# The queries' rotary sine part added in DRAM by accumulating transfers, in a retention and attention block on one core

## The chip, the cores and the metric

The kernel runs on one core of a Trainium2 chip. The metric is the device time of one execution in microseconds (us): the median of three runs is 1068.7 us, the lowest 1065.72, the highest 1070.0. A core has a matrix engine (PE, which loads its weights beside its products, PEld), a vector engine (DVE), an activation engine (ACT), a general engine (POOL) and a queue engine that only issues transfers (SP). Sixteen DMA engines move data between DRAM and the core's memory. POOL can issue transfers too, through a software queue, and of the kernel's transfers only those add to what stands at the destination.

## The reference

One encoder block over 1024 positions and 16 learned tokens ahead of them, in float32. One input projection feeds two branches, and a gated sum of both goes through an output projection and a norm:

```python
u = _rms_norm(h, pre_w)
z = u @ w_in
rq, rk, rv, rg, aq, ak, av, ag, gr, ga = _split_in(z)
...
o_r = _bidirectional_retention(rq, rk, rv, lg_f, lg_b)[:, META_PAD:]
...
o_r = o_r * ret_nw.astype(jnp.float32) * jax.nn.silu(rg.astype(jnp.float32))
y_r = o_r.astype(h.dtype) @ w_rb

aq = _pad_front(_rotary(aq.reshape(B, T, ATT_HEADS, ATT_HD), pos))
ak = _pad_front(_rotary(ak.reshape(B, T, ATT_GROUPS, ATT_HD), pos))
...
o_a = _windowed_sink_attention(aq, ak, av, sink)[:, META_PAD:].reshape(B, T, ATT_Q)
o_a = o_a * jax.nn.silu(ag.astype(jnp.float32))
y_a = o_a.astype(h.dtype) @ w_ab

mix = jax.nn.sigmoid(gr) * y_r + jax.nn.sigmoid(ga) * y_a
out = mix @ w_o
return h + _rms_norm(out, post_w)
```

The change concerns the rotary of the attention's queries, `aq`: 8 heads of 128 channels.

```python
t1, t2 = tf[..., :half], tf[..., half:]
return jnp.concatenate([t1 * cos - t2 * sin, t2 * cos + t1 * sin], axis=-1)
```

Each half of a head's channels, 64 of 128, gets the other half times the sine.

## The kernel before

A float32 product is made of three products of rounded parts: an operand is cast on ACT to its high part, DVE subtracts that from the operand to get the low part, and `mm3` (L94 to L96) issues high x high, low x high and high x low. So nearly every weight tile costs one ACT cast and one DVE subtraction (L110) ahead of its matmuls.

The large projections run in "phases" (class `Phase`). A phase works through units of 256 output channels by 1024 positions, by a scheme of seven products in place of eight (`PROD`): `prepare` makes the sums of weight blocks and splits them (for the first phase in rows of L1011, L1033 and L110, tiles `why`, `wly`, `wry`), `product` issues twelve matmuls into a PSUM bank, `combine` adds the banks' results into four output tiles `c1`, `u2`, `u3`, `c5` of 128x512, and a `post` works on each finished tile.

The stages, in us of the profiled execution: the retention's projections and the retention itself up to about 330; the first phase `y` to about 515, with units 0 and 1, then 16 and 17, 18 and 19 (the attention's queries), then 2 and 3; the attention to 666; and then the phases `z` (remaining gates), `r`, `a` and `o`. In the first phase the posts of units 0 to 3 multiply a gate into the retention's result (`z_post`, L1320, L1330, L1333; it loads the result as tile `v`, L1314), and those of units 16 to 19 are `query_post` (L1443): two DVE products of 64 partitions each write the sine part with its halves swapped into a tile `m2` (L1446, L1447), a third makes the cosine part (L1448), POOL adds the two (L1449), and SP stores the sum to `aq_d` in DRAM (L1451). There are 16 such posts, four for each unit. The attention loads the queries back from `aq_d` (`qf`).

Beside the phases runs helper work that later stages need: single products of "prepared" units (`LATER`: 4, 10, 5, 11, ...), whose weights come by `pre_fetch` (L850, tiles `we`, two of 512 KB), are summed by `pre_sums` (L855; DVE rows L860 to L862) and split by `pre_parts` and `pre_low` (tiles `w_4h`, `w_4l`, `w_10h`, `w_10l`). `gen_pre` makes the products (banks `pe`), copies them to a tile `e` (L885) and stores it; `pre_split` (L814, L822, L825) makes sums of `w_out` as tiles `wT..` and stores them. Tables of numbers set where in the order this work is written down: `FIRST_AT` by steps of the first phase (F is `pre_fetch`, S `pre_sums`, P `pre_parts`, L `pre_low`, then the unit), `BEGUN` by steps of the attention's helper products, `FILL` how many of those stand between the parts of each attention chunk, `REFILL` and `LATE` loads and splits of the last phases. A scheduler with a model of time then orders the instructions of each engine.

Two rings of buffers matter. The ring `g` (`gtile`, 7 tiles of 128x512 in the first phase, 6 later) holds the tiles `v`, `e` and `wT`; `m2` has 2 of its own. The weight tiles `wr` come in two pairs, one in the pool `keep`, one in `lp`; `pre_fetch` takes the pair in `keep`.

A chunk of the attention goes from the scores on PE (`ps`) through DVE (L1523) and ACT (L1526) to POOL, which divides (tile `p`, L1536), and back to PE for transposes (`pt`, L1547) and values (`po`).

Of the kernel before, what the change touches and what calls it, by code (L numbers as in the profile page):

```python
# [7 lines left out]
F32 = mybir.dt.float32  # L8
R = mybir.dt.float32r
AF = mybir.ActivationFunctionType  # L10
ALU = mybir.AluOpType
# [5 lines left out]
P = 128  # L17
# [7 lines left out]
MW = 720  # L25
NC = 2 * NB
START = 4, 12
FILL = ((2, 2),) * 1 + ((2, 1),) * 1 + ((2, 3),) * 2 + ((4, 3),) * 1 + ((2, 3),) * 6 + ((2, 4),) * 1 + ((2, 3),) * 1 + ((2, 4),) * 1 + ((2, 3),) * 1 + ((3, 3),) * 1 + ((2, 1),) * 1 + ((2, 2),) * 1 + ((2, 3),) * 2 + ((2, 4),) * 1 + ((0, 3),) * 1 + ((2, 3),) * 4 + ((3, 3),) * 1 + ((2, 4),) * 1 + ((1, 3),) * 1
EARLY = 8, 9
LATER = 4, 10, 5, 11, 6, 12, 7, 13, 14, 15  # L30
PRE = {u: (2, 3, 5) for u in LATER}
BORDER = 12, 0, 12
LAST = 9
REFILL = -48, 5, 5
LATE = -15, -14, -13, -9, -7, -6, -5, -3, -3, -1

LEADS = 2, 4, 6
VALUES_AT = ((-1, "w1", "s0", "s1"), (1, "l2"), (4, "w0"), (6, "c2"), (8, "n6", "s2", "pT2.0.1.2"),
             (16, "f0", "l3"), (17, "f1", "f2"), (20, "c3", "z"), (21, "s3", "f3"), (22, "pT2.3"))
FIRST_AT = ((1, "k6"), (2, "pT3"), (6, "pT4"), (7, "m4"), (12, "tT3"), (13, "x0"), (14, "tT2", "tT4"),  # L40
# [4 lines left out]

U_QK, U_V, U_G = 0, 4, 8
U_AK, U_AV, U_AQ, U_AG = 12, 13, 14, 18
# [8 lines left out]
def block_kernel(ctx: ExitStack, tc: tile.TileContext, xT, x, meta, w_in, w_rb, w_ab, w_out, vecs, dec, sink,  # L56
                 post_w, rope, tab, out):
    nc = tc.nc
    PSUM = bass.MemoryType.PSUM

    keep = ctx.enter_context(tc.tile_pool(name="keep", bufs=1))
# [37 lines left out]
    def follow(*ins):  # L99

        st = ExitStack()
        for i in ins:
            st.enter_context(tc.issue_after(i))
        return st
# [92 lines left out]
    sr = turn.tile([P, T], F32, name="sr")  # L197
# [320 lines left out]
    z_stack, lp = ExitStack(), None  # L518
# [204 lines left out]
    aq_d = [dram.tile([4, P, SEQ], F32, tag=f"aq{g}", name=f"aq_d{g}") for g in range(2)]  # L723
# [110 lines left out]
    fetched_w, parts = {}, {}  # L834
    spare, e_from, e_bank = [ra], [pj], {}
# [12 lines left out]
            parts[u, 2] = part(h, i), part(l, i)  # L848

    def pre_fetch(u):  # L850
        fetched_w[u] = [keep.tile([P, 4, 256], F32, tag="wr", bufs=2, name=f"we{u}_{j}") for j in range(2)]
        for j, t in enumerate(fetched_w[u]):
            nc.sync.dma_start(t, w_in[gates[u], :, 4 * j:4 * j + 4, :])

# [115 lines left out]
    final = "o", 3, 4  # L970
    sub, mul, add = ALU.subtract, ALU.mult, ALU.add

    staged, gates_ = [2, 6], [7]

    def stage(name, j=0, dt=F32):
        return (yp if j else lp).tile([P, 512], dt, tag=f"sg{int(j)}", bufs=staged[bool(j)], name=name)
# [1 line left out]
    def gtile(name):  # L978
        return gp.tile([P, 512], F32, tag="g", bufs=gates_[0], name=name)
# [205 lines left out]
    def refill(nm, src):  # L1185
# [3 lines left out]
        def load(i, j):  # L1189
            def f():  # L1190
                for k in range(4):
                    x[i, j, k] = t = stage(f"{nm}{i}{j}{k}", j)
                    src(t, 4 * i + k, j)
            return f
# [4 lines left out]
        def plain(n, i, j):  # L1199
            def f():  # L1200
                for k in range(4):
                    split_b(n, k, x[i, j, k])
            return f
# [23 lines left out]
        def early(k):  # L1227
            def f():
                a, b, c, d = (stage(f"{nm}e{i}{j}{k}", j) for i in range(2) for j in range(2))
                for t, (i, j) in zip((a, b, c, d), ((0, 0), (0, 1), (1, 0), (1, 1))):  # L1230
                    src(t, 4 * i + k, j)
                x["e", k] = a, b, c, d
            return f

        def split_early(k):
            def f():
                a, b, c, d = x.pop(("e", k))
                nc.vector.tensor_tensor(a, b, a, sub)
                for n, t in (("T1", a), ("B21", c), ("B22", d)):
                    split_b(n, k, t)  # L1240
            return f
# [10 lines left out]
        if nm == "z":  # L1252
            d = {}
            for i, f in zip(LATE, (load(0, 1), load(1, 1), load(0, 0), t23, plain("B11", 0, 0), load(1, 0),
                                   plain("T2", 1, 1), plain("T3", 0, 1), t4, plain("T4", 1, 0))):
                d.setdefault(i, []).append(f)
            for k in range(4):
                d.setdefault(REFILL[0] + REFILL[1] * k, []).insert(0, early(k))
                d.setdefault(REFILL[0] + REFILL[1] * k + REFILL[2], []).append(split_early(k))
            return d  # L1260
# [181 lines left out]
    ph_o = Phase("o", seq, o_load, o_post, apart=(0, 1))  # L1442
    def query_post(u, i, j, o, to=None):  # L1443
        s, to = half[j], o if to is None else to
        m2 = spare[0].tile([P, 512], F32, tag="m2", bufs=2, name=f"m2_aq{u}{i}{j}")
        nc.vector.tensor_tensor(m2[64:128], o[0:64], sr[0:64, s], mul)  # L1446
        nc.vector.tensor_tensor(m2[0:64], o[64:128], sr[64:128, s], mul)  # L1447
        nc.vector.tensor_tensor(to, o, cr[:, s], mul)  # L1448
        nc.gpsimd.tensor_tensor(to, to, m2, add)  # L1449
        made.add((u, j, i))  # L1450
        nc.sync.dma_start(aq_d[u // 2][2 * (u % 2) + i, :, 512 * j:512 * j + 512], to)  # L1451

    def first_post(u, i, j, o, to=None):
        (query_post if u > 15 else z_post)(u - 16 * (u > 15), i, j, o, to)
# [33 lines left out]
    def attention():  # L1488
# [95 lines left out]
        def fill(n):  # L1584
            owed[0] += n
            while owed[0] > 0:
                cost = next(works, None)
                if cost is None:
                    return
                owed[0] -= cost  # L1590
# [11 lines left out]
        def scores(k):  # L1602
            with follow(*latest, *marks("oa", "lo")):
                stage1(*chunks[k])
            if chunks[k] == (0, 2 * NB - 1):
                keys(1, 0, later_k[0][:, NM:NM + 256], later_k[0][:, 0:NM])
            if chunks[k] == (1, 0):
                keys(1, 1, later_k[0][:, NM + 256:T])
            edge_values(*chunks[k])
# [11 lines left out]
        for k in range(len(chunks)):  # L1621
# [9 lines left out]
            if ends > 0:  # L1631
                with follow(*latest):
                    fill(FILL[k][0])
                scores(k + 2)
                with follow(*latest):
                    fill(FILL[k][1])
            if k:
# [61 lines left out]
    def first_weights(u):  # L1699
        for n in ("A11", "A12"):  # L1700
            first_phase.block(u, n)

    jobs = dict(l=x_load, c=x_scale, s=x_sums, p=x_parts, f=x_first, t=t_store, m=more, n=second_fetch, k=second_parts, x=lambda k: pre_load(k, act_src(w_out)), y=pre_split, A=ready, F=pre_fetch, S=pre_sums, P=pre_parts,
                L=pre_low, z=lambda _: next(first), w=first_weights, r=lambda _: first_phase.raw.clear())

    def at(table):
        return {i: [(jobs[j[0]], *(int(a) if a.isdigit() else a for a in j[1:].split("."))) for j in js]
                for i, *js in table}
# [16 lines left out]
    free[:] = ["pj"] * 3 + ["p1"] * 2 + ["p3"]  # L1725
    table = at(FIRST_AT)
    for n, _ in enumerate(first):
# [9 lines left out]
    vah, val = (atv.tile([P, NB, 256], R, name=n) for n in ("vah", "val"))  # L1737

    BEGUN = {5: [(pre_sums, 5), (pre_fetch, 11)],
             6: [(pre_parts, 5)],  # L1740
             7: [(pre_low, 5)],
             13: [(pre_sums, 11), (pre_fetch, 6)],
             14: [(pre_parts, 11)],
             15: [(pre_low, 11)],
# [2 lines left out]
             23: [(pre_low, 6)],  # L1747
             24: [(load_k,)],
             29: [(pre_sums, 12), (pre_fetch, 7)],
             30: [(pre_parts, 12)],  # L1750
             31: [(pre_low, 12)],
             37: [(pre_sums, 7), (pre_fetch, 13)],
             38: [(pre_parts, 7)],
             39: [(pre_low, 7)],
# [13 lines left out]
    i = attention()  # L1768
# [7 lines left out]
    lp = ctx.enter_context(tc.tile_pool(name="lp", bufs=1, reuse_waits="tile", side="right"))  # L1776
# [105 lines left out]
```

## Time and profile before

| | |
|---|---|
| median of three runs | 1068.7 us (1065.72 to 1070.0) |
| profiled execution, its own time | 1067.16 us |
| its span | 1065.4 us |
| granted PE clock over the span | 0.993 |
| PE, DVE, ACT, POOL busy | 1033.8, 866.9, 510.5, 214.7 us |
| PE idle in 404 to 496, 496 to 532 | 8.62, 7.55 us |
| DVE busy in 404 to 496 | 90.50 of 92 us |
| DMA moved | 212.98 MB, of it 6.82 MB through the software queue |

Rows of instructions give the start, the duration, the engine, the line, the operation, the tiles written and read, and in brackets the idle time ahead of it with what ended it. Rows of waits give the waiting engine and tile, what it waited for, the total, how often, and the longest. Rows of windows give the stretch, its length and the busy time of each engine with the number of instructions, then the granted clock, the share of the DMA engines and GB/s. Rows of groups give shortest, median and longest duration in ns. PE's matmuls overlap, so that one of 0.40 us follows another by 0.23.

### The profile page before, as it was taken

Reading aid. Unit: us, or ns where it says so; the run is one execution under the profiler, and the core shown is the slowest. Engines: PE = TensorE matmul, PEld = TensorE weight load, DVE = VectorE, ACT = ScalarE, POOL = GpSimd, SP = SyncE. Lnnn points to the kernel's source line nnn. Section 1 sums busy time; section 2 is a strip of 40 time slices with the busy share of each in tenths; the row PEclk is TensorE's granted clock in tenths of the full one; section 3 lists DMA queues with packets and bytes.
Section 4 is the critical chain, followed back from the end, with each engine's and each line's share of the span. In section 5 each row is a group of like instructions: output and inputs, shape, how many; then the busy total and the mean of one; then the engine's idle time right before and its main releaser. Section 6 shows DMA issues by size and latency. Waiting matters only on the chain.

```text
span 1065.4 us, 17204 instructions
## 1 busy us (share of the span) xinstructions
PE 1033.8 (97%) x5797; PEld 893.1 (84%) x5797; DVE 866.9 (81%) x1750; ACT 510.5 (48%) x1116; POOL 214.7 (20%) x268
## 2 busy tenths in 40 slices
PE   9999999999999999998799999999999999999996
PEld 7998999989998888776588989788888888787885
DVE  7887778879899689997867886789899799768764
ACT  5541432423435642422567777466557445333443
POOL 3324225344242002221123322000000000111032
PEclk9999999999999999999999999999999999999999
DMA  9322212224343596583867684999989747789364
GB/s 339 150 80 90 99 41 80 80 84 155 100 150 120 183 397 241 186 267 119 294 210 230 210 259 137 351 368 358 319 274 351 259 140 236 217 221 324 98 99 80
DMA packets 115017, 212.98 MB, mean 200 GB/s; under 512 B 12160, under 2 KB 43808, under 8 KB 112304
## 3 DMA queue, kind: packets, MB, share of 16 engines
q1 hardware_dynamic: 111040, 204.78, 55.9%
q0 software_dynamic: 3744, 6.82, 4.4%
q8 instruction: 46, 0.75, 0.3%
q14 instruction: 43, 0.35, 0.1%
q10 hardware_dynamic: 144, 0.27, 0.1%
HBM read 142.57 MB, written 72.93 MB: 202 GB/s over the span
## 4 chain that ended last, share of the span: by engine, by line
PE 80%; DVE 9%; DMA 7%; issue 2%; ACT 1%; POOL 1%; SPq 0%; DVEq 0%; POOLq 0%; ACTq 0%
PE bz L95 5%; PE bz L94 5%; PE bz L96 5%; PE pv L95 3%; PE pv L94 3%; PE pv L96 3%; PE bo L95 2%; PE bo L94 2%; PE br L95 2%; PE bo L96 2%; PE br L94 2%; PE br L96 2%; PE by L95 2%; PE by L96 2%; PE by L94 2%
## 5 line engine op out<-in xcount | busy, mean ns | idle before, releaser
L94 PE MATMUL pv<-wh,big 128*128 128x256 f32 x256 | 73.3, 286 | 0.0
L95 PE MATMUL pv<-wh,big 128*128 128x256 f32 x256 | 72.9, 285 | 0.0
L96 PE MATMUL pv<-wl,big 128*128 128x256 f32 x256 | 72.5, 283 | 0.0
L1536 POOL TENSOR_SCALAR p<-p,den 128x352 f32<-128x352 f32 (+2 forms) x60 | 38.0, 646 | 127.6 <-DVE den L1529 54.8
L1368 POOL DMA_DIRECT2D mx_d<-c1a x4 | 3.7, 920 | 287.0 <-DVE c1a L1359 287.0
L1011 ACT CAST why<-wry 128x512 fp32r<-128x512 f32 x56 | 32.9, 620 | 57.9 <-DVE wry L1033 33.0
L94 PE MATMUL bz<-T,lhz 128*128 128x512 f32 x144 | 56.8, 395 | 0.0
L96 PE MATMUL bz<-T,lhz 128*128 128x512 f32 x144 | 56.8, 394 | 0.0
L95 PE MATMUL bz<-T,llz 128*128 128x512 f32 x144 | 56.8, 394 | 0.0
L94 PE MATMUL by<-big,why 128*128 128x512 f32 x128 | 51.0, 400 | 4.4 <-DVE c5y L1448 4.4
L95 PE MATMUL by<-big,wly 128*128 128x512 f32 x128 | 51.3, 401 | 0.0
L96 PE MATMUL by<-big,why 128*128 128x512 f32 x128 | 50.8, 397 | 0.0
L110 DVE TENSOR_TENSOR wly<-wry,why 128x512 fp32r<-128x512 f32 x56 | 43.7, 802 | 6.3 <-ACT why L1011 6.0
L95 PEld LDWEIGHTS pv<-wh,big 128*128 128x128 f32 x256 | 48.2, 188 | 0.3
L94 PEld LDWEIGHTS pv<-wh,big 128*128 128x128 f32 x256 | 48.2, 188 | 0.2
L96 PEld LDWEIGHTS pv<-wl,big 128*128 128x128 f32 x256 | 48.3, 189 | 0.2
L1526 ACT ACTIVATE p<-raw,nm 128x353 f32<-128x353 f32 (+2 forms) x64 | 36.2, 567 | 20.4 <-DVE nm L1523 19.5
L1523 DVE CUSTOM_DVE_ANT_0 raw<-ps,mask,nsink 128x352 f32<-128x352 f32 (+2 forms) x64 | 33.2, 548 | 3.0 <-ACT p L1526 1.6
L595 ACT ACTIVATE op<-pa,rcol 128x256 f32<-128x256 f32 x32 | 15.2, 476 | 42.0 <-PE pa L96 41.6
L657 ACT ACTIVATE ost<-to,rnw 128x128 f32<-128x128 f32 x64 | 20.0, 365 | 31.4 <-PE to L652 22.1
L687 POOL TENSOR_TENSOR rs<-rs,mhalf 128x1 f32<-128x1 f32 x32 | 23.3, 729 | 52.8 <-DVE rs L686 49.6
L94 PEld LDWEIGHTS by<-big,why 128*128 128x128 f32 x128 | 24.4, 191 | 10.7 <-ACT u2y L1105 4.8
(723 smaller groups left out, 3788.0 us busy)
## 6 DMA issues: line engine op xcount, KB each, us to landing
e<-e SPq DMA_DIRECT2D x60, 256.0 KB, 5.2
we<-in_w_in_dram SPq DMA_DIRECT2D x20, 512.0 KB, 5.1
wr<-in_w_in_dram SPq DMA_DIRECT2D x19, 512.0 KB, 4.3
wry<-in_w_in_dram SPq DMA_DIRECT2D x16, 512.0 KB, 6.4
tg<-tg_d SPq DMA_DIRECT2D x32, 256.0 KB, 5.1
T<-tT SPq DMA_DIRECT2D x6, 1024.0 KB, 10.8
T<-preT SPq DMA_DIRECT2D x6, 1024.0 KB, 7.6
wrz<-in_w_in_dram SPq DMA_DIRECT2D x20, 256.0 KB, 5.5
```

Source lines behind the costliest of these rows:

```text
L94: nc.tensor.matmul(o, ah, bh, start=first, stop=False, **kw)
L95: nc.tensor.matmul(o, al, bh, start=False, stop=False, **kw)
L96: latest[:] = [nc.tensor.matmul(o, ah, bl, start=False, stop=last, **kw).ins]
L110: return nc.vector.tensor_tensor(o, i, hi.bitcast(F32), ALU.subtract).ins
L595: nc.scalar.activation(o, pa[:, 0:256], AF.Copy, scale=rcol[:, c:c + 1])
L657: nc.scalar.activation(ost[0][:, e_, w0:w0 + P], to[:, P * e_:P * e_ + P], AF.Copy, scale=rnw[:, 2 * h + e_:2 * h + e_ + 1])
L687: nc.gpsimd.tensor_tensor(rs, rs, mhalf[:, 0:1], ALU.pow)
L1011: nc.scalar.copy(h, src)
L1368: nc.gpsimd.dma_start(d, to, accum_op=ALU.add)
L1523: nc.vector.tensor_tensor_reduce(raw[e_][:, 1:1 + wid], s[:, 0:wid], mask[:, mo:mo + wid], -SCALE, nsink[:, hp:hp + 1], ALU.add, ALU.min, ...
L1526: last["exp"] = nc.scalar.activation(p[:, 0:1 + wid], raw[e_][:, 0:1 + wid], AF.Exp, scale=-1.0, bias=nm_[:, e_:e_ + 1], accum_out=den[:, ...
L1536: nc.gpsimd.tensor_scalar(pt[e_][:, 0:wid], pt[e_][:, 0:wid], den[:, e_:e_ + 1], 1.0, op0=ALU.mult, op1=ALU.mult)
```

## The change

`query_post` now makes the sine part unswapped, in one DVE product over 128 partitions, into a tile of the ring `g`. The cosine part is stored to `aq_d` as soon as DVE has made it. POOL then issues two accumulating transfers of 64 partitions (128 KB) each, which add the upper half of the sine part to the lower half in DRAM and the other way round. POOL's adds are gone. The ring `g` has 9 tiles in the first phase. Unit 10's weights go into the pair `wr` of the pool `lp`, and are fetched beside unit 4's; the helper tables are renumbered.

```diff
-FILL = ...
+FILL = ...
-REFILL = -48, 5, 5
-LATE = -15, -14, -13, -9, -7, -6, -5, -3, -3, -1
+REFILL = -48, 6, 5
+LATE = -15, -14, -12, -9, -7, -6, -5, -3, -3, -1
...
-            (37, "y2.3"), (44, "A0"), (47, "m4"), (49, "r", "F4"), (51, "S4", "P4", "A1"),
-            (52, "L4", "F10", "A2"), (53, "A3"), (54, "m4", "S10", "P10", "L10", "F5"))
+            (37, "y2.3"), (44, "A0"), (47, "m4"), (49, "r", "F4", "F10"), (51, "S4", "P4", "A1"),
+            (52, "L4", "F5", "A2"), (53, "S10", "P10", "A3"), (54, "m4", "L10"))
...
     def pre_fetch(u):
-        fetched_w[u] = [keep.tile([P, 4, 256], F32, tag="wr", bufs=2, name=f"we{u}_{j}") for j in range(2)]
+        pool = lp if u == LATER[1] else keep
+        fetched_w[u] = [pool.tile([P, 4, 256], F32, tag="wr", bufs=2, name=f"we{u}_{j}") for j in range(2)]
...
-    staged, gates_ = [2, 6], [7]
+    staged, gates_ = [2, 6], [9]
...
     def query_post(u, i, j, o, to=None):
         s, to = half[j], o if to is None else to
-        m2 = spare[0].tile([P, 512], F32, tag="m2", bufs=2, name=f"m2_aq{u}{i}{j}")
-        nc.vector.tensor_tensor(m2[64:128], o[0:64], sr[0:64, s], mul)
-        nc.vector.tensor_tensor(m2[0:64], o[64:128], sr[64:128, s], mul)
+        m2 = gtile(f"m2_aq{u}{i}{j}")
+        nc.vector.tensor_tensor(m2, o, sr[:, s], mul)
         nc.vector.tensor_tensor(to, o, cr[:, s], mul)
-        nc.gpsimd.tensor_tensor(to, to, m2, add)
         made.add((u, j, i))
-        nc.sync.dma_start(aq_d[u // 2][2 * (u % 2) + i, :, 512 * j:512 * j + 512], to)
+        d = aq_d[u // 2][2 * (u % 2) + i, :, 512 * j:512 * j + 512]
+        nc.sync.dma_start(d, to)
+        for a, b in ((slice(0, 64), slice(64, P)), (slice(64, P), slice(0, 64))):
+            nc.gpsimd.dma_start(d[a], m2[b], accum_op=ALU.add)
...
-             30: [(pre_parts, 12)],
-             31: [(pre_low, 12)],
+             30: [(pre_parts, 12), (pre_low, 12)],
```

`FILL`, 32 pairs long, differs in four of them; not shown are two moves in `FIRST_AT`, "tT4" from step 14 to 12 and "k8" from 31 to 27.

PE has the same 5728 rows in another order, DVE 16 fewer, and POOL 32 transfers for 16 adds. The first place is DVE at the last three query posts of units 18 and 19. Before (`m_aq` is `m2`, `by` the bank, `wly` low parts of weights):

```order
L1446 TENSOR_TENSOR m_aq_6203<-by_1_5896,sr 64x512
L1447 TENSOR_TENSOR m_aq_6203<-by_1_5896,sr 64x512
L1448 TENSOR_TENSOR c5y_6202<-by_1_5896,cr 128x512
L110 TENSOR_TENSOR wly_6_6211<-wry_0_6129,why_6_6210 128x512
L110 TENSOR_TENSOR wly_7_6255<-wry_0_6102,why_7_6254 128x512
L1448 TENSOR_TENSOR u2y_6016<-u2y_6016,cr 128x512
L110 TENSOR_TENSOR wly_7_6255<-wry_0_6129,why_7_6254 128x512
L110 TENSOR_TENSOR wly_4_6294<-wry_1_6159,why_4_6293 128x512
L110 TENSOR_TENSOR wly_4_6294<-wry_1_6185,why_4_6293 128x512
L1446 TENSOR_TENSOR m_aq_6227<-by_1_5923,sr 64x512
L1447 TENSOR_TENSOR m_aq_6227<-by_1_5923,sr 64x512
L1448 TENSOR_TENSOR c5y_6226<-by_1_5923,cr 128x512
```

And now, with the same posts:

```order
L1447 TENSOR_TENSOR m_aq_6203<-by_1_5900,sr 128x512
L1448 TENSOR_TENSOR c5y_6202<-by_1_5900,cr 128x512
L110 TENSOR_TENSOR wly_5_6163<-wry_0_6129,why_5_6162 128x512
L1034 TENSOR_TENSOR wry_0_6102<-wry_0_6102 128x512
L1448 TENSOR_TENSOR u2y_6016<-u2y_6016,cr 128x512
L1447 TENSOR_TENSOR m_aq_6227<-by_1_5927,sr 128x512
L1448 TENSOR_TENSOR c5y_6226<-by_1_5927,cr 128x512
```

The posts now stand ahead of the splits of products 6, 7 and 4 of units 2 and 3, which stood among them.

The second place is SP's queue at the end of the query posts, up to the weights of unit 10 (6499 before, 6430 and 6431 now; unit 4's are 6426 and 6427). Before:

```order
L1451 DMA aq_d_587<-u2y_5997 128x512
L1451 DMA aq_d_587<-c5y_6202 128x512
L1451 DMA aq_d_587<-u2y_6016 128x512
L1451 DMA aq_d_587<-c5y_6226 128x512
L853 DMA we_0_6426<-in_w_in_dram 128x1024
L1304 DMA wx_7556<-in_w_out_dram 128x512 x2
L853 DMA we_1_6427<-in_w_in_dram 128x1024
L1304 DMA wx_7559<-in_w_out_dram 128x512 x2
L863 DMA s_4_100<-we_1_6427 128x512
L853 DMA we_0_6499<-in_w_in_dram 128x1024
```

And now:

```order
L1451 DMA aq_d_587<-c5y_6226 128x512
L1315 DMA v_6356<-oTr_d 128x512
L887 DMA e_2_94<-e_2_6373 128x512
L1315 DMA v_6395<-oTr_d 128x512
L1315 DMA v_6421<-oTr_d 128x512
L854 DMA we_0_6426<-in_w_in_dram 128x1024
L887 DMA e_2_97<-e_2_6578 128x512
L854 DMA we_0_6430<-in_w_in_dram 128x1024
L854 DMA we_1_6427<-in_w_in_dram 128x1024
L854 DMA we_1_6431<-in_w_in_dram 128x1024
```

Unit 10's weights are fetched among unit 4's, the loads `wx` come later, and loads of `v` and stores of `e` now stand between the last query store and the fetch. Through the ring `g`, the loads of `v` wait for accumulating transfers that read the buffer before.

The third place is ACT in the last products of units 2 and 3, before:

```order
L1105 COPY u2y_6354<-by_1_6258 128x512
L1011 CAST why_3_6398<-wry_1_6159 128x512
L1011 CAST why_3_6398<-wry_1_6185 128x512
L1105 COPY u3y_6388<-by_1_6236 128x512
L1105 COPY u3y_6414<-by_1_6258 128x512
L790 CAST w_4h<-we_0_6426 128x1024
```

and now:

```order
L1106 COPY u2y_6354<-by_1_6258 128x512
L1012 CAST why_2_6338<-wry_1_6185 128x512
L886 COPY e_2_6578<-pe_2_6565 128x512
L1012 CAST why_3_6398<-wry_1_6159 128x512
L1012 CAST why_3_6398<-wry_1_6185 128x512
L1106 COPY u3y_6388<-by_1_6236 128x512
```

The copy of the result `e_2_6578` now stands ahead of the casts of `why_3`; its buffer of the ring `g` is the one that the last query post's sine part leaves, so it waits for the last accumulating transfer.

More of the change, by code (lines that the diff above doesn't have):

```diff
@@ L27 @@
 START = 4, 12
-FILL = ((2, 2),) * 1 + ((2, 1),) * 1 + ((2, 3),) * 2 + ((4, 3),) * 1 + ((2, 3),) * 6 + ((2, 4),) * 1 + ((2, 3),) * 1 + ((2, 4),) * 1 + ((2, 3),) * 1 + ((3, 3),) * 1 + ((2, 1),) * 1 + ((2, 2),) * 1 + ((2, 3),) * 2 + ((2, 4),) * 1 + ((0, 3),) * 1 + ((2, 3),) * 4 + ((3, 3),) * 1 + ((2, 4),) * 1 + ((1, 3),) * 1
+FILL = ((2, 2),) * 1 + ((3, 1),) * 1 + ((2, 3),) * 1 + ((2, 2),) * 1 + ((4, 3),) * 1 + ((2, 3),) * 6 + ((2, 4),) * 1 + ((2, 3),) * 1 + ((2, 4),) * 1 + ((2, 3),) * 1 + ((3, 3),) * 1 + ((2, 1),) * 1 + ((2, 2),) * 1 + ((2, 3),) * 2 + ((2, 4),) * 1 + ((0, 4),) * 1 + ((2, 2),) * 1 + ((2, 3),) * 3 + ((3, 3),) * 1 + ((2, 4),) * 1 + ((1, 3),) * 1
 EARLY = 8, 9
@@ L39 @@
              (16, "f0", "l3"), (17, "f1", "f2"), (20, "c3", "z"), (21, "s3", "f3"), (22, "pT2.3"))
-FIRST_AT = ((1, "k6"), (2, "pT3"), (6, "pT4"), (7, "m4"), (12, "tT3"), (13, "x0"), (14, "tT2", "tT4"),
+FIRST_AT = ((1, "k6"), (2, "pT3"), (6, "pT4"), (7, "m4"), (12, "tT3", "tT4"), (13, "x0"), (14, "tT2"),
             (16, "y0.0"), (17, "y0.1"), (18, "y0.2"), (19, "y0.3", "x1"), (23, "y1.0"), (24, "m4", "y1.1"),
[3 rows of a table removed]
[3 rows of a table added]
 U_QK, U_V, U_G = 0, 4, 8
```

2 rows, old and new, of the table FIRST_AT are left out of this document.

## The prediction

> **What bounds the kernel now.** I read the page's busy times and chain first, then the windows stage by stage, then the waits, and last the rows around the longest waits.
>
> ```profile
> PE 1033.8 (97%) x5797; PEld 893.1 (84%) x5797; DVE 866.9 (81%) x1750; ACT 510.5 (48%) x1116; POOL 214.7 (20%) x268
> PE 80%; DVE 9%; DMA 7%; issue 2%; ACT 1%; POOL 1%; SPq 0%; DVEq 0%; POOLq 0%; ACTq 0%
> 404.00:496.00 92.00, 83.38 (x350) 65.81 (x349) 90.50 (x118) 28.91 (x51) 25.05 (x16) 0.98 0.57 193
> 496.00:532.00 36.00, 28.45 (x125) 22.28 (x124) 26.21 (x52) 16.18 (x31) 2.64 (x4) 0.95 0.81 272
> 536.00:666.00 130.00, 127.96 (x817) 115.41 (x816) 97.88 (x261) 93.25 (x255) 34.90 (x56) 1.00 0.66 206
> 666.00:990.00 324.00, 322.33 (x1394) 260.00 (x1393) 274.08 (x448) 168.51 (x305) 10.61 (x12) 1.00 0.84 283
> ```
>
> The window rows give length, then busy time of PE, PEld, DVE, ACT and POOL, the granted clock, the DMA share and GB/s. From 666 to 990 PE stands still for 1.67 us of 324, and in the attention for 2.04 of 130: the end moves one for one with PE, and there is nothing to win there. From 404 to 496, the stretch of the query posts, the roles change: DVE is busy for 90.50 of 92 us and PE idles for 8.62. From 496 to 532, the hand-over to the attention, PE idles for 7.55 more. After the two longest pauses the clock falls as well:
>
> ```profile
> 488.00:492.00 4.00, 0.56 (x1) 0.34 (x2) 3.94 (x7) 0.58 (x1) 0.59 (x2) 0.88 0.18 66
> 492.00:496.00 4.00, 4.00 (x14) 3.21 (x14) 3.86 (x5) 1.17 (x2) 1.02 (x1) 0.69 0.30 95
> 528.00:532.00 4.00, 1.66 (x6) 1.10 (x7) 3.10 (x10) 2.59 (x10) 2.64 (x4) 0.57 0.97 335
> 532.00:536.00 4.00, 4.00 (x16) 3.52 (x15) 3.19 (x8) 2.90 (x7) 0.46 (x1) 0.57 0.99 351
> 486.67 0.40 PE L94 MATMUL by<-big,why 128*128 128x512 f32 x1
> 491.44 0.76 PE L94 MATMUL by<-big,why 128*128 128x512 f32 x1 [4.38 <-DVE c5y L1448]
> PE by L94 <- DVE c5y L1448: 4.4, 1, 4.4
> PE by L95 <- DVE wly L110: 4.2, 4, 2.1
> PE pe L95 <- DVE w_10l L110: 2.4, 1, 2.4
> ```
>
> The work lost to the clock is busy time x (1 - clock): 1.2 us in 492 to 496 (4.00 x 0.31), 0.7 in 528 to 532 and 1.7 in 532 to 536. So 8.62 + 1.2 = 9.8 us can be won before 496, and 7.55 + 2.4 = 10.0 us in the hand-over. Nothing else in the kernel is within reach of this change.
>
> **What the posts cost DVE.** Sixteen query posts run here.
>
> ```profile
> L1446 DVE TENSOR_TENSOR m_aq<-c1y,sr x4: 685/685/1284, 401.7 to 456.0; 64x512 f32<-64x512 f32 x4
> L1447 DVE TENSOR_TENSOR m_aq<-c1y,sr x4: 686/687/689, 402.4 to 456.7; 64x512 f32<-64x512 f32 x4
> L1448 DVE TENSOR_TENSOR c1y<-c1y,cr x4: 683/684/693, 403.7 to 460.4; 128x512 f32<-128x512 f32 x4
> 413.01 0.68 DVE L1446 TENSOR_TENSOR m_aq<-u3y,sr 64x512 f32<-64x512 f32 x1
> 413.71 1.69 DVE L1447 TENSOR_TENSOR m_aq<-u3y,sr 64x512 f32<-64x512 f32 x1
> 413.12 1.74 POOL L1449 TENSOR_TENSOR u3y<-u3y,m_aq 128x512 f32<-128x512 f32 x1 [4.00 <-issue]
> L1449 POOL TENSOR_TENSOR u3y<-u3y,m_aq x4: 1290/1678/1741, 413.1 to 471.7; 128x512 f32<-128x512 f32 x4
> 405.02 1.28 DVE L1446 TENSOR_TENSOR m_aq<-c1y,sr 64x512 f32<-64x512 f32 x1
> 404.47 1.29 POOL L1449 TENSOR_TENSOR c1y<-c1y,m_aq 128x512 f32<-128x512 f32 x1 [57.57 <-DVE c1y L1448]
> ```
>
> (1) A product over 64 partitions lasts as long as one over 128 (0.685 beside 0.684). One instruction for two therefore takes 16 x 0.69 = 11 us off DVE. (2) Where a POOL add runs, the DVE instruction that meets it ends with it: 0.6 us late at 405.02, 1.0 at 413.71. At these two ends the 16 adds cost DVE 9.6 to 16 us. I take 15, because the adds' median is nearer to 413.12 than to 404.47 (1678 ns in the row of u3y). DVE then needs some 90.5 - 26 = 64 us where PE needs 82, so it stops being the bound by a wide margin, even at the low end (70).
>
> (3) New on POOL: 32 accumulating transfers instead of 16 adds. The nearest rows are those of the later stages, over 256 KB.
>
> ```profile
> 933.23 1.15 POOL L1368 DMA_DIRECT2D mx_d<-c5a  x1
> 933.58 0.69 DVE L1045 TENSOR_TENSOR sta2S<-sta2S,wra 128x512 f32<-128x512 f32 x1
> L1368 POOL DMA_DIRECT2D mx_d<-c1a x4: 865/869/1075, 921.5 to 964.5; - x4
> DMA to landing us min/median/max: 4.1/5.5/7.0
> 1014.04 0.89 POOL L1426 DMA_DIRECT2D out_dram<-c1o  x1 [1.76 <-DVE c1o L1425]
> 1024.95 1.12 POOL L1426 DMA_DIRECT2D out_dram<-u2o  x1
> out_dram<-u2o POOLq DMA_DIRECT2D x2, 256.0 KB, 7.5
> q0 software_dynamic: 1152, 2.10, 49.2%
> ```
>
> POOL's share is 32 x 0.87 = 28 us against 25.05 now, on an engine with nothing else to do there. If each issue held up a DVE row for the 0.87 us that it lasts, those 28 us would come back on DVE, which would then be as full as now. But the DVE row beside the issue at 933.23 keeps its 0.69, so I cost the issues at nothing for DVE. The last row (window 1010 to 1040: packets, MB, share) says that 8 such transfers took 0.492 x 30 = 14.8 us of all 16 DMA engines, 1.85 us per 256 KB. Sixteen posts add 30 us of it to the 0.57 x 92 = 52 us used from 404 to 496. That is 82 us in a stretch that shrinks to about 83: full, and a rival below. Bounds: nothing, if packets of two queues overlap within an engine, to 30 us.
>
> (4) The hand-over. Today it hangs on the end of the posts:
>
> ```profile
> aq_d<-c5y SPq DMA_DIRECT2D x4, 256.0 KB, 2.0
> 490.60 0.69 DVE L1448 TENSOR_TENSOR c5y<-by,cr 128x512 f32<-128x512 f32 x1
> 493.05 0.32 SPq L1451 DMA_DIRECT2D aq_d<-c5y  x1
> 495.75 0.38 SPq L853 DMA_DIRECT2D we<-in_w_in_dram  x1
> 502.51 0.69 DVE L860 TENSOR_TENSOR we<-we,we 128x512 f32<-128x512 f32 x1 [6.30 <-DMA we<-in_w_in_dram]
> 514.57 0.39 PE L96 MATMUL by<-big,why 128*128 128x512 f32 x1
> 526.10 0.43 DVE L1523 CUSTOM_DVE_ANT_0 raw<-ps,mask,nsink 128x208 f32<-128x208 f32 x1
> 530.07 0.47 PE L1547 MATMUL pt<-ident,p 128*128 128x128 f32 x1 [2.42 <-POOL p L1536]
> ```
>
> PE had finished the last query product 73 matmuls before 486.67, at 83.38 / 350 = 0.24 us apiece at about 469; DVE's last post came 21 us later. Of PE's 8.62 idle us some 4 lie before that (all but the 4.38 at c5y), so without them the last product ends at 465, and the last L1448, two DVE rows on, at about 467. The new chain from there: the store issues 2.4 us later (490.60 to 493.05), the row of aq_d gives 2.0 us for it to land, two issues take 1.7, the accumulate 5.5. So its buffer is free at about 478.7. The order of ACT puts the copy of the last prepared result (e_2_6578), which takes that buffer, ahead of the casts of why_3, and SP fetches the second half of unit 4's weights only after wly_3: copy, two casts and two subtractions, all of 128x512, cost 5 x 0.69 = 3.4 us, the fetch 6.8 (495.75 to 502.51). The sum at `we` then starts near 489 instead of 502.5, and PE's y products end near 506 instead of 514.8. The lead of the sum over that end grows from 12.3 to some 17 us, and unit 10's weights, in their own buffers, come with unit 4's, which takes away the 2.4 us on w_10l. Up to the whole 10.0 us can go; none of it goes if SP's loads, which now wait for accumulates, use the lead up. I take half, 5.0, since the posts of units 2 and 3 remain between `we` and the first softmax. What is late next is the softmax of the first chunk (526.10 to 530.07, 4 us), which nothing here shortens.
>
> The Trainium skill's page "DMA: Bandwidth & Descriptors", section "Anatomy of one DMA — SWDGE (gpsimd) path", fits 2.0 us plus bytes over 436 GB/s per software transfer, an estimate of 2.3 us for 128 KB. The rows of this kernel say 4.1 at the least for 256 KB, where that fit gives 2.6. By the fit the buffer would be free 3.2 us earlier and the sum would read 1051; I stay with the rows.
>
> (5) The other edits (BEGUN, FILL, REFILL, LATE, k8 and tT4 moved) reorder helpers in stages where PE idles by 1 to 2%. I cost them at 0, plus or minus 1.5 us; their cover is PE's saturation, and if it fails the waits of those stages (2.04 + 1.67) could about double.
>
> **Sum.** Before 496: 9.8 us less 1.4 that I leave for waits on ACT and on loads, -8.4 (bounds -6 and -9.8). Hand-over -5.0 (bounds +1 and -10.0). Rest 0. Together -13.4 on the profiled execution's 1067.16, so 1053.8, say 1054. The median of the three runs is 1068.7 and they span 4.3 us; half a percent, 5.3 us, is about what a measurement can tell from no change, so "faster" means under 1063.4.
>
> **Rivals.** A: the hand-over stays as long as it is. For it: SP's queue gains waits for accumulates (v loads, the e stores) ahead of the fetches. Against: 13 us of lead. Only the first term remains: 1067.2 - 8.4 = 1058.8.
>
> B: the DMA engines take DVE's place as the bound. For it: 82 of 83 us, and the share is already 0.97 to 0.99 in 528 to 536. Against: weight loads run ahead by several units, and 0.57 leaves 40 us. If a third of the 30 us shows up on PE, the gain falls to 13.4 - 10 = 3 us: 1064; about 1062 in the middle.
>
> C, slower: the last accumulate lands late. Then ACT stands at the copy e_2_6578 with the casts of why_3 and the copies of u3y behind it, and SP without wly_3 can't fetch. Each us of delay eats one of the gain: none is left at 13 us (landing at 492), and slower by half a percent starts at 13.4 + 5.3 = 19. If software transfers ran one at a time at the 4.1 us of the fastest row, 32 would take 131 us from about 408 (404.47 and a store), end at 539, 60 us late and give 1067 + 47 = 1114; at half that price they end at 474, in time, so it decides from some 2.5 us each. Against: eight of 256 KB issued between 1014.04 and 1024.95 had landed within 7.5 us of the last, 18.4 us for eight, 1.15 per 128 KB, 37 us for 32.
>
> The Trainium skill's page "SBUF — State Buffer", section "Who interferes with whom", says that GpSimd's descriptor writing is starved while DVE runs in a 2-port mode. By this rule C would come about; but the page gives tensor_tensor no such mode, and DVE's rows in this stretch are TENSOR_TENSOR, so I add nothing to C's chance for it.
>
> **Chances.** As forecast (1047 to 1058) 0.56; A (1056 to 1061) 0.17; B (1059 to 1067) 0.15; C (1068 and more) 0.09; something else 0.03. Faster: 0.55 + 0.16 + 0.08 = 0.79. Same: 0.10. Slower: 0.11. The range for eight in ten reaches from the full gain, 1067 - 19.8 = 1047, through A into the middle of B: 1047 to 1063.
>
> **What would show it.** Right: from 404 to 490 DVE under 80% busy with no row of 1.69 in it, PE without the pause before the c5y bank and the clock at 1.00; the `we` sum near 489, the first softmax near 512. Wrong: PE or DVE waiting on accumulates of aq_d (A, C), ACT idle at the copy of e for more than 5 us (C), a DMA share near 1.0 with PE waiting for wly whose wry is late (B), or DVE rows of 1.0 us beside L1453's issues (term 3).

## The result and the profile after

The changed kernel takes 1052.11 us (median of six runs, 1050.0 to 1055.06), the kernel before 1068.43 us in six runs beside it: a ratio of 0.9854, 95% interval 0.9834 to 0.9874, or 15.6 us less by that ratio (the two medians differ by 16.3). The forecast was 1054, with 1047 to 1063. On another chip, beside the last experiments, the ratio was 0.9847 (0.9833 to 0.9860). The profiled execution has a span of 1049.7 us against 1065.4.

The busy times and the chain of the changed kernel's page:

```profile
PE 1030.0 (98%) x5797; PEld 893.0 (85%) x5797; DVE 842.1 (80%) x1734; ACT 511.0 (49%) x1116; POOL 217.5 (21%) x284
PE 86%; DVE 5%; DMA 5%; issue 1%; SPq 1%; ACT 1%; POOL 0%; DVEq 0%; POOLq 0%; ACTq 0%
```

Its windows over the first phase's second half, the hand-over to the attention, the attention and the phases after it, then three shorter ones, columns as before:

```profile
404.00:496.00 92.00, 92.00 (x401) 74.94 (x400) 70.83 (x113) 32.43 (x57) 27.26 (x32) 1.00 0.96 270
496.00:532.00 36.00, 31.08 (x151) 25.68 (x150) 28.70 (x65) 21.60 (x49) 6.46 (x10) 0.91 0.79 270
520.00:650.00 130.00, 128.56 (x819) 116.90 (x817) 99.33 (x263) 93.78 (x254) 35.25 (x56) 0.99 0.67 208
650.00:974.00 324.00, 322.29 (x1395) 259.96 (x1394) 274.21 (x449) 168.61 (x307) 10.45 (x12) 1.00 0.84 283
404.00:482.00 78.00, 78.00 (x340) 63.47 (x339) 61.39 (x99) 27.79 (x49) 27.26 (x32) 1.00 1.01 278
512.00:516.00 4.00, 1.06 (x6) 0.83 (x6) 2.14 (x10) 3.51 (x8) 0.57 (x1) 0.91 0.94 316
516.00:520.00 4.00, 3.41 (x11) 2.65 (x12) 3.27 (x9) 2.73 (x6) 2.58 (x4) 0.50 0.97 361
```

From 404 to 496 PE is busy throughout, at full clock, with 401 matmuls where there were 350. DVE falls from 90.50 to 70.83 us. The DMA engines are full: share 1.01 up to 482. What is left stands in the last two rows: PE runs out of work at about 510 and its clock falls.

The chain that the prediction followed, in the timelines of DVE, POOL, ACT, SP, DVE and PE of the changed kernel (start, duration, what; `e` is the result of a second product, that is, product 2 of the seven of a prepared unit, and the later of the two copies is that of e_2_6578):

```profile
465.15 0.69 DVE L1448 TENSOR_TENSOR u2y<-u2y,cr 128x512 f32<-128x512 f32 x1
465.75 0.68 DVE L1447 TENSOR_TENSOR m_aq<-by,sr 128x512 f32<-128x512 f32 x1
466.35 0.68 DVE L1448 TENSOR_TENSOR c5y<-by,cr 128x512 f32<-128x512 f32 x1
...
465.29 1.68 POOL L1453 DMA_DIRECT2D aq_d<-m_aq  x2 [0.92 <-DVE wry L1034]
474.43 3.41 POOL L1453 DMA_DIRECT2D aq_d<-m_aq  x4 [2.46 <-DMA aq_d<-u2y]
...
476.75 0.59 ACT L886 COPY e<-pe 128x512 f32<-128x512 f32 x1 [5.68 <-issue]
482.31 0.59 ACT L886 COPY e<-pe 128x512 f32<-128x512 f32 x1 [0.24 <-PE pe L96]
...
483.88 1.81 SPq L854 DMA_DIRECT2D we<-in_w_in_dram  x3
...
492.43 0.69 DVE L861 TENSOR_TENSOR we<-we,we 128x512 f32<-128x512 f32 x1 [3.09 <-DMA we<-in_w_in_dram]
512.05 0.43 DVE L1525 CUSTOM_DVE_ANT_0 raw<-ps,mask,nsink 128x208 f32<-128x208 f32 x1
...
503.98 0.39 PE L96 MATMUL by<-big,why 128*128 128x512 f32 x1
512.54 0.40 PE L94 MATMUL ps<-kTh,aqh 128*128 128x288 f32 x1 [1.93 <-DVE nm L1525]
516.32 0.47 PE L1549 MATMUL pt<-ident,p 128*128 128x128 f32 x1 [2.72 <-POOL p L1538]
```

The last post ends at 467 as forecast; the sum at `we` starts at 492.43 (forecast 489, before 502.51), the first softmax at 512.05 (forecast 512, before 526.10). Three marks on PE divide the gain: the y products end at 504.4 and not 515.0 (-10.6 us), the first transposes start at 516.32 and not 530.07 (another -3.2), and the attention's last product starts at 660.88 and not 676.05 (another -1.4). The rest up to the 15.7 of the span, 0.5, lies in the phases after it.

### The profile page after: what moved, and what is told of

Its sections match the earlier page's. It is cut to its first block, busy times and chain, and to the rows that moved or that the text cites. A ratio compares the mean times of both kernels' runs of the same rounds, so it can differ in the third digit from the quotient of the medians.

```text
span 1049.7 us, 17233 instructions
## 1 busy us (share of the span) xinstructions
PE 1030.0 (98%) x5797; PEld 893.0 (85%) x5797; DVE 842.1 (80%) x1734; ACT 511.0 (49%) x1116; POOL 217.5 (21%) x284
## 3 DMA queue, kind: packets, MB, share of 16 engines
q1 hardware_dynamic: 111040, 204.78, 56.9%
## 4 chain that ended last, share of the span: by engine, by line
PE 86%; DVE 5%; DMA 5%; issue 1%; SPq 1%; ACT 1%; POOL 0%; DVEq 0%; POOLq 0%; ACTq 0%
PE bz L95 5%; PE bz L94 5%; PE bz L96 5%; PE by L95 4%; PE by L96 4%; PE by L94 4%; PE pv L95 3%; PE pv L94 3%; PE pv L96 3%; PE bo L95 3%; PE bo L94 3%; PE br L95 2%; PE bo L96 2%; PE br L94 2%; PE br L96 2%; PE ba L95 2%
## 5 line engine op out<-in xcount | busy, mean ns | idle before, releaser
L1453 POOL DMA_DIRECT2D aq_d<-m_aq x32 | 27.3, 1277 | 102.6 <-DVE u3y L1448 65.9
L110 DVE TENSOR_TENSOR wly<-wry,why 128x512 fp32r<-128x512 f32 x56 | 37.9, 693 | 12.1 <-ACT why L1012 11.9
```

The lines of the kernel that those rows point to most:

```text
L110: return nc.vector.tensor_tensor(o, i, hi.bitcast(F32), ALU.subtract).ins
L1453: nc.gpsimd.dma_start(d[a], m2[b], accum_op=ALU.add)
```

## The experiments

Two theories were set against each other first. By the first, relieving DVE in the stretch of the query posts is what wins, and the tables are small change. By the second, the tables and unit 10's own buffers carry a third or more. For each run the table gives the ratio to the kernel before, run beside it, and from its profile, in us, the end of the y products and the starts of the sum at `we`, the first softmax, the first transposes and the attention's last product. The runs were spread over several chips, so the ratios are what to compare, not the medians.

| kernel | median, us | ratio (95%) | y end | `we` | softmax | transposes | attention's last |
|---|---|---|---|---|---|---|---|
| before | 1068.43 | 1 | 515.0 | 502.5 | 526.1 | 530.1 | 676.1 |
| change | 1052.11 | 0.9854 (0.9834-0.9874) | 504.4 | 492.4 | 512.1 | 516.3 | 660.9 |
| post alone | 1060.41 | 0.9940 (0.9918-0.9961) | 503.9 | 496.0 | 515.7 | 523.6 | 670.5 |
| rest alone | 1066.98 | 0.9991 (0.9977-1.0006) | 515.0 | 501.2 | 526.5 | 529.9 | 673.8 |
| two products | 1062.07 | 0.9957 (0.9944-0.9970) | 509.4 | 500.0 | 521.5 | 526.3 | 671.1 |
| shared buffer | 1053.43 | 0.9871 (0.9856-0.9886) | 502.4 | 489.7 | 511.0 | 518.5 | 661.6 |
| post and k8 | 1056.82 | 0.9898 (0.9877-0.9919) | 502.9 | 489.7 | 511.0 | 518.4 | 664.8 |
| no sine | 1050.86 | 0.9841 (0.9811-0.9870) | 503.0 | 491.4 | 510.2 | 513.9 | 660.4 |
| own e | 1054.74 | 0.9877 (0.9858-0.9897) | 504.3 | 495.8 | 515.4 | 519.2 | 662.5 |
| more bytes | 1056.04 | 0.9892 (0.9855-0.9929) | 503.1 | 496.6 | 515.6 | 520.6 | 666.1 |
| START 18 | 1061.66 | 0.9948 (0.9930-0.9966) | 503.6 | 490.3 | 510.0 | 514.2 | 669.8 |
| START 14 | 1059.42 | 0.9930 (0.9918-0.9942) | 503.1 | 492.2 | 511.8 | 516.1 | 667.9 |
| change again | 1050.62 | 0.9847 (0.9833-0.9860) | 503.8 | 491.1 | 510.7 | 515.0 | 659.7 |
| old attention tables | 1052.16 | 0.9873 (0.9857-0.9889) | 502.5 | 491.6 | 511.2 | 515.5 | 662.5 |

### The post alone, and the rest alone

The first takes the kernel before and puts in the new `query_post` and the ring of 9, nothing else. The second takes the change and puts back:

```diff
-    staged, gates_ = [2, 6], [9]
+    staged, gates_ = [2, 6], [7]
...
-        m2 = gtile(f"m2_aq{u}{i}{j}")
-        nc.vector.tensor_tensor(m2, o, sr[:, s], mul)
+        m2 = spare[0].tile([P, 512], F32, tag="m2", bufs=2, name=f"m2_aq{u}{i}{j}")
+        nc.vector.tensor_tensor(m2[64:128], o[0:64], sr[0:64, s], mul)
+        nc.vector.tensor_tensor(m2[0:64], o[64:128], sr[64:128, s], mul)
         nc.vector.tensor_tensor(to, o, cr[:, s], mul)
+        nc.gpsimd.tensor_tensor(to, to, m2, add)
...
-        for a, b in ((slice(0, 64), slice(64, P)), (slice(64, P), slice(0, 64))):
-            nc.gpsimd.dma_start(d[a], m2[b], accum_op=ALU.add)
```

> The kernel before with the new query post and the ring of 9 alone; tables and buffers as before. Theory 1 (relieving DVE in the stretch of the query posts is what wins): PE stands still for under 1 us from 404 to 490, and 12 to 15 of the 16 us are there, 1053 to 1057. Theory 2 (the tables and unit 10's own buffers carry a third or more of the gain): 1058 to 1063, with the wait for the weights of unit 10 back in the hand-over.

> The change without its query post: POOL adds, two products of 64 partitions, ring of 7 and m2 as before, but unit 10's own buffers and all new tables. Theory 1: DVE stays full from 404 to 496 and PE keeps its pause at the c5y bank; 1065 to 1070. Theory 2: 1058 to 1063.

Neither theory holds as it was put. The post alone brings 0.6% and the rest alone 0.1% (an interval that holds 1), where both bring 1.5%. Windows of the post alone, then of the rest alone:

```profile
404.00:496.00 92.00, 92.00 (x401) 74.90 (x400) 67.44 (x109) 31.57 (x55) 27.31 (x32) 1.00 0.95 265
496.00:540.00 44.00, 30.64 (x134) 24.61 (x133) 31.15 (x68) 21.68 (x48) 4.48 (x8) 0.81 0.74 254
```

```profile
404.00:496.00 92.00, 83.50 (x349) 65.78 (x348) 88.81 (x118) 28.75 (x51) 24.46 (x16) 0.98 0.57 187
```

The first phase is settled by the post: with it PE is full up to 496 and the y products end 11 us earlier, without it DVE is. But the post alone loses 4.6 of these 11 us by the first transposes. Where, its SP, DVE and PE timelines and a row of SP's waits (480 to 510) show:

```profile
504.00 0.32 SPq L886 DMA_DIRECT2D e<-e  x1
505.98 0.33 SPq L853 DMA_DIRECT2D we<-in_w_in_dram  x1
...
512.52 0.69 DVE L860 TENSOR_TENSOR we<-we,we 128x512 f32<-128x512 f32 x1 [2.37 <-DMA we<-in_w_in_dram]
...
516.88 0.80 PE L94 MATMUL pe<-big,w_10h 128*128 128x512 f32 x1 [7.37 <-ACT w_10h L790]
...
SPq L1314 <- DMA aq_d<-m_aq: 9.4, 2, 7.7
```

On SP the store of the last second product's result stands ahead of the second fetch of unit 10's weights. They are summed at 512.52, and PE stands 7.4 us at their first product, with the scores of the second chunk queued behind it. The store itself held SP up for only 1.2 us; the fetch behind it waited another 1.6 for the split of unit 4's weights, whose buffers it takes. Unit 4 was late already: its fetches stand behind loads of `v` that waited 9.4 us for accumulating transfers, and its sum at `we` starts at 496.0.

### One table entry, and the tables of the attention

```diff
-            (26, "y1.2"), (27, "y1.3", "n8"), (28, "x2"), (31, "y2.0", "k8"), (33, "y2.1"), (35, "y2.2"),
+            (26, "y1.2"), (27, "y1.3", "n8", "k8"), (28, "x2"), (31, "y2.0"), (33, "y2.1"), (35, "y2.2"),
```

on top of the post alone. `k8` splits the weights of the last two second products.

> The new query post and the ring of 9 as in the run of the post alone, and of the tables only k8 (the split of the weights for the last two second products) moved from step 31 to 27. In that program the store of the last second product's result stands on SP ahead of the second fetch of unit 10's weights no more. Theory 3 (the post alone lost 7 us because that store held up unit 10's weights, and PE's queue stood for 7.4 us at its product with the scores behind it): 1052 to 1056, and PE's wait for w_10h under 3 us. Rival (FILL and the other tables of the attention bring the 7 us): 1059 to 1061, as with the post alone.

1056.82, the ratio 0.9898 against 0.9940: this one entry is worth about 4.5 us once the post is in, though the two intervals just touch. The first transposes come 5 us earlier, and PE's waits for w_10 shrink to 1.2 and 1.8 us. So the entry brings about half of the 9 us between the post alone and the change. That it does so by freeing the store, as theory 3 has it, is not shown: unit 10's sum comes 11.7 us earlier (500.81), but unit 4's at `we` already comes 6.3 earlier (489.7), and which share the store has was not separated.

For the other half, the change with the old FILL, REFILL, LATE and BEGUN was run, the change itself beside it:

> The change with FILL, REFILL, LATE and BEGUN as before; FIRST_AT, the buffers and the query post are the change's. If these tables carry a part of the gain (the program with post and k8 alone waited 3.5 us from 540 to 660 where the change waits 1.4): 1053.5 to 1056. If they are worth nothing, as the prediction costed them: 1050 to 1053.5.

> The change once more, beside the others on one chip: 1050 to 1055.

The old tables give 0.9873, the change 0.9847: some 2.7 us by the ratios, nearly all of it after the first transposes (515.5 and 515.0, then 662.5 and 659.7). The size is loose: the intervals overlap, the medians differ by 1.5 us, and 1052.16 lies in the range that was set for tables worth nothing. The sign is firmer: each of the four executions with the old tables (1051.72 at the least) took longer than each of the four of the change (1051.38 at the most).

### Unit 10's buffers

The change with unit 10's weights back in the pair of unit 4 and their steps as before.

```diff
-        pool = lp if u == LATER[1] else keep
-        fetched_w[u] = [pool.tile(
+        fetched_w[u] = [keep.tile(
...
-            (49, "r", "F4", "F10"), (51, "S4", "P4", "A1"),
-            (52, "L4", "F5", "A2"), (53, "S10", "P10", "A3"), (54, "m4", "L10"))
+            (49, "r", "F4"), (51, "S4", "P4", "A1"),
+            (52, "L4", "F10", "A2"), (53, "A3"), (54, "m4", "S10", "P10", "L10", "F5"))
```

> The change, but unit 10's weights take the pair of buffers of unit 4 again, with their steps as before. Theory 1: only the hand-over loses, by the wait for w_10l, 2 to 3 us: 1053 to 1056. Theory 2: 1057 or more. If unit 10's weights are not on the way at all: 1051 to 1053.

0.9871 against 0.9854 for the change: 1 to 2 us, but the intervals overlap, so it may be nothing. Theory 1's mechanism is there: PE waits for w_10 again (1.7 and 1.8 us, none in the change) and the transposes come 2.2 us later; by the attention's last product 0.7 of that is left.

### Products or meetings

The change, but with the halves swapped on DVE and one accumulating transfer of 128 partitions:

```diff
-        nc.vector.tensor_tensor(m2, o, sr[:, s], mul)
+        nc.vector.tensor_tensor(m2[64:128], o[0:64], sr[0:64, s], mul)
+        nc.vector.tensor_tensor(m2[0:64], o[64:128], sr[64:128, s], mul)
...
-        for a, b in ((slice(0, 64), slice(64, P)), (slice(64, P), slice(0, 64))):
-            nc.gpsimd.dma_start(d[a], m2[b], accum_op=ALU.add)
+        nc.gpsimd.dma_start(d, m2, accum_op=ALU.add)
```

> The change, but DVE makes the sine part in two products of 64 partitions with the halves swapped, and one accumulating transfer of 128 partitions (256 KB) adds it; the bytes stay, POOL issues 16 transfers and not 32. DVE has its 11 us back but no meeting with a POOL add. Theory 1 in the form that the meetings (15 us) suffice to free PE: DVE at about 82 us where PE needs 80 to 82, so 1052 to 1057. Rival, that the 16 fewer products are needed as well: DVE stays the bound and PE waits again, 1058 to 1064.

1062.07, so the meetings alone don't suffice. Two windows, the second up to the end of the posts:

```profile
404.00:496.00 92.00, 88.39 (x377) 71.57 (x376) 76.46 (x119) 30.78 (x54) 14.13 (x16) 0.98 0.93 248
404.00:484.00 80.00, 80.00 (x348) 64.96 (x346) 74.48 (x116) 26.42 (x46) 12.37 (x14) 1.00 0.94 254
```

The ACT timeline, where PE's first long stop comes from:

```profile
486.73 0.59 ACT L886 COPY e<-pe 128x512 f32<-128x512 f32 x1 [9.06 <-DMA aq_d<-m_aq]
490.91 0.59 ACT L886 COPY e<-pe 128x512 f32<-128x512 f32 x1 [1.58 <-DMA aq_d<-m_aq]
```

Up to 484 PE is never idle, and DVE is busy for 74 of 80 us: nearly full, but PE doesn't wait for it. The time is in the rival's range (1058 to 1064), by another way than the rival's. The posts end at 480 (467 in the change), the last transfers are issued at 484.85 and after (474.43 in the change), and ACT stands 9 us at the copy of `e` for one of them, with the copies out of the y banks and the casts behind it; PE stops for 3.6 us and `we` comes at 500.0. This is the prediction's rival C in small: a late accumulate costs by the copy of `e`. One thing stays open: here the transfers are also twice as large, and how much of the lateness is theirs and how much the posts' was not separated.

### What the transfers cost

Three runs: the change without the two accumulating transfers (the sine part is left out); the change with every cosine part stored a second time to a place that nobody reads; and the change with a buffer of their own for the second products' results, a tile of the ring `g` given up for it.

```diff
-        for a, b in ((slice(0, 64), slice(64, P)), (slice(64, P), slice(0, 64))):
-            nc.gpsimd.dma_start(d[a], m2[b], accum_op=ALU.add)
```

> The change without its 32 accumulating transfers: the sine part is made and left out, so the result is not the reference's. It measures what the transfers cost. Theory 1 (they are hidden, though DMA stands at 1.0 from 404 to 482): 1048 to 1053, all of the difference in the hand-over. Rival (the full DMA engines hold up loads that PE waits for): 1044 or less.

```diff
         nc.sync.dma_start(d, to)
+        nc.sync.dma_start(more_d[u // 2][2 * (u % 2) + i, :, 512 * j:512 * j + 512], to)
```

> The change with each post's cosine part stored a second time, to a place that nobody reads: 16 x 256 KB, some 12 us more of all 16 DMA engines from 404 to 490, where they are full already. If DMA is the next bound there (rival B of the prediction): 4 to 12 us slower than the change, 1056 to 1064. If the loads have slack beyond the 30 us of the accumulating transfers: 1051 to 1055.

```diff
-        o = gtile(f"e{u}_{p}") if spare[0] is zq else
+        o = gp.tile([P, 512], F32, tag="eo", bufs=1, name=f"e{u}_{p}") if spare[0] is zq else
```

> The change with a buffer of their own for the results of the last second products in place of one of the ring's 9 (8 + 1), so ACT's copy of them waits for no accumulating transfer and the casts behind it don't either. If the copies held the hand-over up: ACT's wait of 5.7 us at the first copy is gone, the sum at we starts some 2 us earlier, 1048 to 1051. If the fetch is held by the loads of v and the weights' own buffers: 1050 to 1053.

Without the transfers the ratio is 0.9841 and the DMA share from 404 to 496 falls from 0.96 to 0.68. The change's 0.9854 can't be told from that, at an interval of some 3 us to either side: to that measure the transfers are hidden. The 4.2 MB more of the second run should take some 12 us of the DMA engines, an estimate by the change's plain transfers (19.65 MB in 56.9 us from 404 to 490). Its windows read:

```profile
404.00:496.00 92.00, 92.00 (x400) 74.94 (x400) 66.21 (x107) 31.36 (x55) 27.34 (x32) 1.00 1.01 293
496.00:540.00 44.00, 36.46 (x173) 29.94 (x172) 34.97 (x77) 24.19 (x53) 6.46 (x10) 0.88 0.86 294
```

PE is still full up to 496, with the share at 1.01 where it was 0.96; so some 5 us of the added transfers lie in this stretch, the rest behind it. The ratio stands about 4 us above the change's, with an interval of nearly 4 us to either side; the median of 1056.04 is at the lower edge of what was expected if DMA were the next bound. The loss is in the hand-over, though: `we` at 496.6, the transposes at 520.6. So a full DMA stretch doesn't hold PE's weights up here; what comes late is the fetch at its end. The buffer of their own for the results made things no better (0.9877, `we` at 495.8): the copies waited for no transfer, but the sum at `we` waited 6.5 us for its fetch, issued on SP from 486.56 on. Ahead of it stand the loads of `v`, whose ring has one buffer less; they waited for accumulating transfers (SP's waits from 470 to 500):

```profile
SPq L1315 <- DMA aq_d<-m_aq: 13.4, 6, 3.3
```

### More work ahead of the first softmax

PE's rest of idle time in the change lies before the first transposes, so more of the helper products were put there: the second number of START says how many steps of them stand ahead of the second chunk's scores.

```diff
-START = 4, 12
+START = 4, 18
```

and 4, 14.

> The change with START = 4, 18: nine matmuls more of the helper products (2.1 us) stand on PE ahead of the scores of the second chunk, which wait 1.9 us for the first softmax in the change, and as many fewer at the end of the attention. Theory (the hand-over's rest is PE without work before the first softmax): 1049.5 to 1051.5, with the wait at those scores gone and the one at the first transposes kept. Rival (PE only shifts its idle time to the transposes or to later chunks, as the tables were balanced): 1051.5 to 1054.

> The same with START = 4, 14, three matmuls more (0.7 us). Theory: 1051 to 1052, a third of the effect above. Rival: 1051.5 to 1054.

Both are slower than the change, by more than the rival gave: 1061.66 and 1059.42. The larger one does win the hand-over: PE is busy for 21.83 us from 496 to 520 and keeps its clock (19.79 and 0.87 in the change on that chip). The attention loses it again. The attention's window with START 18, then its waits there:

```profile
520.00:650.00 130.00, 121.93 (x755) 109.13 (x755) 92.76 (x245) 88.94 (x238) 35.25 (x54) 0.99 0.65 198
```

```profile
DVE we L861 <- DMA we<-in_w_in_dram: 10.1, 3, 4.6
PE pt L1549 <- DVE pal L110: 4.8, 3, 2.2
```

And those of the change on the same chip:

```profile
520.00:650.00 130.00, 128.65 (x824) 116.71 (x822) 99.15 (x265) 95.04 (x258) 35.11 (x56) 1.00 0.67 205
```

```profile
DVE we L861 <- DMA qf<-aq_d: 3.3, 1, 3.3
PE pt L1549 <- DVE pal L110: 1.1, 2, 0.9
```

The helper products carry the fetches and sums of the next weights with them (BEGUN counts them). Advanced, the sums stand on DVE before their weights have landed, 10.1 us in three waits, and what the transposes need (`pal`) stands behind them. No version here that computes the whole result beats the change.

## Why the prediction was right

**DVE as the bound (terms 1 and 2).** Right, and too small: -8.4 us was forecast to the end of the y products, -10.6 came. The 1.4 us left for waits on ACT and on loads were not needed: PE is busy for all 92. The idle time and the clock were counted, 9.8 us. But 350 matmuls took the place of 401, which is 51 x 92 / 401 = 11.7 us: the 1.9 us beyond are not idle time in the rows. They are slow steps that count as busy. Matmuls follow one another by 0.23 us; the seven from 491.44 on do so by 0.33 to 0.56, which is 1.5 us where the clock sum gave 1.2, and at the other stops the last one before and the first ones after take 0.10 to 0.17 more each, some 1.3 us together. DVE's busy time fell by 24.8 us over the whole span (866.9 to 842.1), where 26 was forecast. In the window it fell by only 19.7, because other work moved up into it: 113 instructions stand there, where 118 less 16 would be 102. One reading was off without effect on the sum: a DVE row that meets a POOL add outlasts it by 0.54 us (413.71 + 1.69 against 413.12 + 1.74) and doesn't end with it.

**The issues cost DVE nothing (term 3).** Right. The DVE rows at 465.15, 465.75 and 466.35 run beside the pair of issues that starts at 465.29, and last 0.69 and 0.68; the first reads two tiles, the others a bank and a tile. No DVE row of 128x512 from 404 to 490 has a mean over 0.70. The Trainium skill's page "SBUF — State Buffer", section "Who interferes with whom", has a DVE instruction with two SBUF inputs contend with a GpSimd instruction that reads SBUF, but not with one that only writes it; the adds before (1.69) and the issue beside the row at 465.15 (0.69) agree with it, if an issue only writes there, which no run here shows.

**The transfers' own time.** The size was right, the place too. The software queue of the changed kernel over 404 to 490 (packets, MB, share), and its line's landing time:

```profile
q0 software_dynamic: 2560, 4.20, 32.8%
DMA to landing us min/median/max: 3.5/6.1/9.6
```

0.328 x 86 = 28.2 us of all 16 engines, 30 forecast. Landing took 6.1 us at the median where 5.5 was taken for twice the bytes; the fit that the page "DMA: Bandwidth & Descriptors" of the Trainium skill gives (section "Anatomy of one DMA — SWDGE (gpsimd) path"), an estimate of 2.3 us, is far below every one of them (3.5 at the least). Rival B, DMA as the bound, had its condition met (1.01) and not its effect: PE had no wait up to 508.

**The hand-over (term 4).** The price was too high: -5.0 forecast, -3.2 measured to the first transposes. The chain was right in part. The last copy of `e`, at 482.31, waited for its product, where the prediction had it wait for the last accumulating transfer. It was the copy before it, at 476.75, that waited 5.7 us for an accumulate, and through it and the loads of `v` the accumulates held SP up ahead of the fetch (SP's waits from 470 to 500):

```profile
SPq L887 <- ACT e L886: 4.6, 1, 4.6
SPq L1315 <- DMA aq_d<-m_aq: 3.6, 2, 2.0
```

The lead of `we` over the end of the y products did not grow to 17 us, it went from 12.5 to 12.0. The sum came 3.4 us later than forecast: the fetch of the second half of unit 4's weights was issued at about 484.5 where 482.2 follows from the prediction, and took 7.9 us, not 6.8. The store took longer as well (5.1 us at the median where 2.0 was taken). One of the prediction's signs against itself thus came about, ACT idle at the copy of `e` for more than 5 us (rival C), and DVE stood 6.1 us for the casts behind it, without making PE wait: its weights were ahead. Rival C is a mechanism that exists: with two products the wait is 9.1 us and PE stops.

**The rest at nothing (term 5).** This is the step that failed, and it is hidden in a good sum. The tables were costed at 0 plus or minus 1.5. With the post in, k8 is worth about 4.5 us and the attention's tables some 2.7; without it, all tables and the buffers together are worth 0.1%. Why they are worth nothing without the post was not separated; that DVE's lateness covered what they move fits the rest alone, where the y products end at 515.0 as before. Without the tables and unit 10's own buffers the change would have come 6 us above the forecast of 1054, inside its range but at rival A: the post alone stands at 1060, with a hand-over that got longer (19.7 us from the end of the y products to the transposes, 15.1 before) and with what rival A names, SP's queue waiting for accumulates ahead of the fetches. That the sum came within some 2 us is in part luck: two terms were too small, by 2.2 (before 496) and 1.9 (the rest, 1.4 and 0.5), and one too large, by 1.8 (the hand-over).

## What to carry to other kernels

When an engine off the matrix engine's path fills a stretch completely, count the matmuls of that stretch, not the idle time, to see what it costs. A relief there moves the next wait to the nearest queue that issues in order: look at what stands ahead of which fetch, since one table entry decided here over half as much as the whole relief. And an accumulating transfer can take an addition, with a swap of partitions, off two engines; here its cost was below what the runs could measure, though in-order queues did wait for its buffers. Look at what stands behind those waits.

## What was not expected of the hardware

A stretch of 78 us with the DMA engines at a share of 1.01 brought PE no wait, and with some 5 us of transfers more between 404 and 496 it still had none there. An accumulating transfer of 128 KB took as long to land as one of 256 KB (6.1 us at the median in the change, 5.3 in the run with two products), with the DMA engines near full in both; halving it did not bring it home earlier here.
